# One block of 512 weight columns instead of two of 256 in the first mixer's input projection

## The chip, the cores and the metric

The kernel runs on one core of one Trainium2 chip. Five engines work side by side, each on a queue of its own, in order: PE multiplies matrices (its weight loads are shown apart as PEld), DVE and ACT work element by element, POOL does small odd jobs, SP issues the loads from memory. They wait for one another by semaphores. The metric is the device time of one execution in microseconds; lower is better. Three runs of the kernel before took 1702.97, 1701.64 and 1698.35 us.

## The reference: what is computed

Two layers of a transformer-like trunk over 512 latent and 256 context tokens, width 1024. Each layer is a mixer and a gated feed-forward part, with a normalisation and a shift, scale and gate that come from a conditioning vector ("modulation"). The mixer of layer 0 multiplies the tokens `h` (768 x 1024) by one weight matrix and cuts the result up:

```python
gq, gk, gv, gog, gz, aq, ak, av = _split(h @ w_in, EVEN_SIZES)   # 256 256 512 512 32 512 128 128 columns
# four heads of chunked gated linear attention, in two directions, on gq gk gv gog gz
dirs.append(_directional_scan(q, k, v, g, n_ctx, reverse=(d == 1)))
# and ordinary attention with normalised queries and keys on aq ak av
qa = _rms(aq.reshape(B, N, ATT_KV_HEADS, ATT_GROUP, ATT_HEAD_DIM), att_q_norm)
ka = _rms(ak.reshape(B, N, ATT_KV_HEADS, ATT_HEAD_DIM), att_k_norm)
o_blocks = lax.map(lambda qb: _softmax_attend(qb, k_all, va), q_blocks)
```

The change touches the second half of `aq` (256 columns) and `ak` with `av` (together 256 columns), which lie side by side in the matrix.

## The kernel before, in words

Tokens lie in tiles of 128; tiles 0 to 3 are latent, 4 and 5 context. `even_mixer` is written as a set of generators ("jobs"), each of which does one step when its name comes up in a string of names that `run` walks through (lines 1215 to 1220). The order of PE's instructions in this part is the order of that string: with `self.pinned` set, every matmul is recorded as one that keeps its place (`pin`, line 348). The other engines' queues are put in order by the scheduler, which may move an instruction ahead of others that wait.

The matrix product keeps single precision by splitting both operands in a high and a low part. A block of weights comes in as units of 1024 numbers per partition (`unit`, line 761): a load into a tile `raw` (three buffers), a cast on ACT that makes the high part `wH` (line 769), and a subtraction on DVE that makes the low part `wL` (line 770). There are four buffers of `wH` and four of `wL` for the whole mixer. `nat_units` (line 795) makes the units of a block of columns, `gemm_nat` (line 801) multiplies two token tiles by it: for each of the eight pieces of the inner dimension three matmuls (`h` high by `wH`, `h` high by `wL`, `h` low by `wH`), 48 in all, into a PSUM tile named `nat`. 256 columns need two units of four pieces each.

The job `q` makes the 256 columns of queries that are left, `kv` the keys and values. Each begins with a step that only makes its units, and then has three steps of 48 matmuls, for the tiles 4 and 5, 0 and 1, 2 and 3; after each, ACT copies PSUM to `natq` or `natk` (lines 1138 and 1141). The other names that matter here:

- `v0`, `v1`, `qk0`, `qk1`, `g0`, `g1`: other blocks of the same product. `v0` comes just ahead of `q`; `qk1` (PSUM tile `gqk1`, units of 128 columns) just behind `kv`.
- `m`: the modulation (`mod_vec`, line 515). DVE adds up `macc` from sixteen loaded pieces `mraw`, two instructions each (line 537); then PE sums over partitions (`mod_acc`), DVE copies the sum (`modrows`, line 469), PE turns it (`modT`), DVE adds a bias (`modcol`, line 481). The first of the two rounds goes on: DVE makes `gc` (line 644), PE turns that (`gcT`), DVE copies it (`gt`).
- `c0`: the first job of the gated linear attention, over the context (`gla_job` and `scan`, lines 1256 and 911). It starts with copies and products into `arrg` (lines 1264 to 1267), then goes through levels 1, 2, 4, ... 64: ACT copies a half of `arrg` into `qkg` of that level (line 976), DVE multiplies the half by a decay (line 981), and the next level follows. PE's `pcg` matmuls read the levels 1, 2 and 4 in a first step of `c0`, and 8 and 16 in a second. In names with numbers, `qkg041`, `qkg048` and `qkg0416` are the levels 1, 8 and 16 of this job. `l0` is the same over the latent tokens (`arrg00`).
- `p`: the preparation of queries and keys for attention (`att_prep`), on ACT, DVE and POOL, from `natq` and `natk`.

## Time and profile before

| | us |
|---|---|
| median of three runs | 1701.64 |
| profiled execution | 1703.25 |
| its span in the trace | 1701.1 |
| PE busy | 1650.1 |
| DVE busy | 1309.1 |
| ACT busy | 921.3 |
| mean clock granted to PE | 0.994 |

PE is busy in 97% of the span. Matmuls are pipelined, so a row's duration is longer than the distance to the next matmul: the 128x256 matmuls of `nat` take 0.285 us each and come 0.12 us apart. The chain of waits is read from the end of the program back to its start, at each step to what released it. Stretches where PE has idle time are few; the part of the program that the change touches lies between 95 and 165 us.

### The profile page before, as it was taken

The page shows a single profiled execution, that of the slowest core. Times are in us where ns is not written, and L with a number is a line of the kernel's source. Part 1 is how long each engine was busy: PE and PEld are TensorE (multiplying, and loading weights), DVE is VectorE, ACT ScalarE, POOL GpSimd, SP SyncE. Part 2 cuts the span into 40 slices and gives each one's busy share as a digit, 9 for nine tenths or more (in the row PEclk, how much of TensorE's full clock was granted, in tenths as well). Part 3 has the DMA queues.
Part 4 walks back from the last instruction along what each step waited for, and adds up shares of the span by engine and source line. Part 5 has one row for each costly group of instructions (what it writes and reads, how often), then busy time and mean ns, then how long its engine had stood idle before and what let it go on. Part 6 is the DMA issues. An engine that isn't in the chain of part 4 may idle for free.

```text
span 1701.1 us, 32534 instructions
## 1 busy us (share of the span) xinstructions
PE 1650.1 (97%) x13407; PEld 1484.4 (87%) x13407; DVE 1309.1 (77%) x2102; ACT 921.3 (54%) x1563; POOL 123.2 (7%) x129
## 2 busy tenths in 40 slices
PE   6999998999999999999997999999999999999997
PEld 5899987888999999998886888988888899999875
DVE  5889677976898988777767618788775499987977
ACT  4745567846544444445456326666564565555654
POOL 1004110011000000003101000000000100000221
PEclk9999999999999999999999999999999999999999
DMA  9651012164243454349535612111114334333793
GB/s 327 191 153 40 2 37 90 51 216 158 85 125 111 136 173 142 100 139 197 99 128 194 210 50 63 51 51 51 52 56 156 124 107 118 112 100 100 193 191 136
DMA packets 184736, 204.79 MB, mean 120 GB/s; under 512 B 7142, under 2 KB 141836, under 8 KB 184588
## 3 DMA queue, kind: packets, MB, share of 16 engines
q1 hardware_dynamic: 173632, 181.82, 34.2%
q0 software_dynamic: 9024, 17.30, 5.9%
q10 hardware_dynamic: 1932, 3.59, 0.6%
q8 instruction: 105, 1.72, 0.4%
q14 instruction: 43, 0.35, 0.1%
HBM read 193.23 MB, written 9.46 MB: 119 GB/s over the span
## 4 chain that ended last, share of the span: by engine, by line
PE 81%; DVE 8%; ACT 4%; DMA 3%; issue 2%; POOL 1%; DVEq 0%; SPq 0%; POOLq 0%; ACTq 0%
PE nat L355 12%; PE a L355 11%; PE ff L355 8%; PE E L355 7%; PE x L355 6%; PE oproj L355 6%; PE b L355 4%; PE D L355 4%; PE o L355 4%; PE fq L355 3%; PE gqk L355 2%; PE pearly L355 2%; PE S L355 2%; PE poh L355 1%; PE attO L355 1%
## 5 line engine op out<-in xcount | busy, mean ns | idle before, releaser
L355 PE MATMUL nat<-wH,x 128*128 128x256 f32 (+2 forms) x968 | 224.5, 321 | 3.0 <-ACT x L735 2.6
L355 PEld LDWEIGHTS nat<-wH,x 128*128 128x128 f32 x968 | 162.6, 190 | 19.6 <-ACT x L735 3.7
L824 ACT CAST wH<-raw 128x1024 fp32r<-128x1024 f32 x120 | 125.0, 1051 | 96.5 <-DVE raw L849 33.6
L825 DVE TENSOR_TENSOR wL<-raw,wH 128x1024 fp32r<-128x1024 f32 x120 | 145.6, 1221 | 20.9 <-ACT wH L824 20.3
L355 PE MATMUL nat<-wL,x 128*128 128x256 f32 (+2 forms) x484 | 153.5, 317 | 0.0
L770 DVE TENSOR_TENSOR wL<-raw,wH 128x1024 fp32r<-128x1024 f32 (+1 forms) x83 | 98.7, 1198 | 49.5 <-ACT wH L769 48.5
L355 PE MATMUL ff<-x,wH 128*128 128x512 f32 (+1 forms) x512 | 127.7, 340 | 0.0
L668 POOL TENSOR_TENSOR rs<-ms,neghalf 128x1 f32<-128x1 f32 (+2 forms) x62 | 65.3, 1058 | 785.5 <-DVE ms L666 785.4
L769 ACT CAST wH<-raw 128x1024 fp32r<-128x1024 f32 (+1 forms) x83 | 84.6, 1034 | 67.8 <-PE ff L355 19.8
L355 PE MATMUL oproj<-wH,x 128*128 128x512 f32 x320 | 102.2, 396 | 0.5 <-ACT x L1288 0.4
L355 PEld LDWEIGHTS nat<-wL,x 128*128 128x128 f32 x484 | 92.3, 191 | 5.9 <-DVE wL L770 0.3
L597 DVE SCALAR_TENSOR_TENSOR macc<-mraw,scT,macc 128x1024 f32<-128x1024 f32 x70 | 88.3, 1280 | 11.6 <-DMA mraw<-in_mod_w_dram 11.2
L355 PEld LDWEIGHTS ff<-x,wH 128*128 128x128 f32 x512 | 87.2, 190 | 10.0
L355 PE MATMUL x<-wH,two 128*128 128x512 f32 x280 | 90.5, 392 | 0.9 <-DVE y L1783 0.7
L976 ACT COPY qkh<-arr 128x512 f32<-128x512 f32 x112 | 70.0, 642 | 36.5 <-DVE arr L981 32.1
L1708 POOL DMA_DIRECT2D t<-in_ffn_w_down_dram x36 | 41.8, 1230 | 649.4 <-DVE wL L1742 610.3
L355 PE MATMUL ff<-x,wL 128*128 128x256 f32 (+1 forms) x256 | 86.2, 337 | 0.0
L849 DVE TENSOR_TENSOR raw<-raw 128x512 f32<-128x512 f32 x120 | 82.8, 690 | 2.8
L981 DVE TENSOR_TENSOR arr<-arr,f 128x512 f32<-128x512 f32 x112 | 74.2, 687 | 1.9 <-ACT qkh L976 0.3
L355 PE MATMUL E<-x,wH 128*128 128x384 f32 (+1 forms) x320 | 70.9, 311 | 0.0
L355 PEld LDWEIGHTS oproj<-wH,x 128*128 128x128 f32 x320 | 59.5, 188 | 12.8 <-ACT x L1288 1.0
L355 PE MATMUL b<-x,wH 128*128 128x384 f32 (+1 forms) x320 | 70.5, 309 | 0.0
(422 smaller groups left out, 4548.5 us busy)
## 6 DMA issues: line engine op xcount, KB each, us to landing
mraw<-in_mod_w_dram SPq DMA_DIRECT2D x80, 512.0 KB, 4.5
raw<-in_ffn_w_gate_dram SPq DMA_DIRECT2D x44, 512.0 KB, 4.6
raw<-in_ffn_w_up_dram SPq DMA_DIRECT2D x44, 512.0 KB, 4.1
raw<-in_odd_w_in_dram SPq DMA_DIRECT2D x40, 512.0 KB, 3.8
t<-in_ffn_w_down_dram POOLq DMA_DIRECT2D x30, 512.0 KB, 7.4
raw<-in_ffn_w_down_dram SPq DMA_DIRECT2D x28, 512.0 KB, 7.2
mraw<-in_mod_w_dram SPq DMA_DIRECT2D x32, 256.0 KB, 6.3
raw<-in_even_w_in_dram SPq DMA_DIRECT2D x16, 512.0 KB, 4.0
```

What stands on the lines that cost most here:

```text
L355: return self.pin(self.nc.tensor.matmul(*a, **k))
L597: nc.vector.scalar_tensor_tensor(a, u, w, a, op0=ALU.mult, op1=ALU.add)
L668: nc.gpsimd.tensor_tensor(rs, ms, self.neghalf.to_broadcast([P, w]), op=ALU.pow)
L769: nc.scalar.copy(H[:, :m], raw[:, :m])
L770: nc.vector.tensor_tensor(L[:, :m], raw[:, :m], H[:, :m].bitcast(F32), op=ALU.subtract)
L824: self.nc.scalar.copy(H, f)
L825: self.nc.vector.tensor_tensor(L, f, H.bitcast(F32), op=ALU.subtract)
L849: add = lambda o, x, y: nc.vector.tensor_tensor(o, x, y, op=ALU.add)
L976: nc.scalar.copy(qkv[:, :, :, half, :], dst)
L981: nc.vector.tensor_tensor(dst, dst, tb, op=ALU.mult)
L1708: add = lambda o, src: self.pin(nc.gpsimd.dma_start(out=o, in_=src, accum_op=ALU.add))
```

## The change

The jobs `q` and `kv` become one job `Q` of 512 columns. Its block needs four units of two pieces each instead of two and two of four, and it has three steps of 48 matmuls of 512 columns in place of six steps of 48 matmuls of 256. After each step ACT makes both copies. In the string of names, `Q` stands where `q` stood for the first time (its units) and three more times; `kv` is gone.

```diff
-        def nat(c0, evac):
+        def nat(c0, evac, n=256):
-            us = self.nat_units(w, c0, 256, 0) + self.nat_units(w, c0, 256, 1)
+            us = self.nat_units(w, c0, n, 0) + self.nat_units(w, c0, n, 1)
             yield
             for t0 in tiles:
-                self.gemm_nat(w, c0, 256, h, (t0,), evac, us=us)
+                self.gemm_nat(w, c0, n, h, (t0,), evac, us=us)
                 yield

-        def ev_q(t0, pt):
+        def ev_qkv(t0, pt):
             nc.scalar.copy(q_part(1)[:, t0 : t0 + 2], pt[:, :, :256].rearrange("p t (m e) -> p t m e", m=4))
-
-        def ev_kv(t0, pt):
-            nc.scalar.copy(natk[:, t0 : t0 + 2, :], pt[:, :, :256])
+            nc.scalar.copy(natk[:, t0 : t0 + 2, :], pt[:, :, 256:])

-            "q": lambda: nat(1536 + 288, ev_q), "kv": lambda: nat(1536 + 544, ev_kv), "m": lambda: mods,
+            "Q": lambda: nat(1536 + 288, ev_qkv, 512), "m": lambda: mods,

-        run("qk0 qk0 e m qk0 e e v0 qk0 e e m qk0 e e m v0 e e m m q v0 m m v0 m m kv q m m q m q m m m m m m m m m qk1 kv m")
+        run("qk0 qk0 e m qk0 e e v0 qk0 e e m qk0 e e m v0 e e m m Q v0 m m v0 m m Q m m m m Q m m m m m m m m qk1 m")
         tp.release()
         gp = self.open_pool("gla")
-        run("c0 l0 kv m c0 kv c0 v1 qk1 c0 p p qk1 c0 l0 p qk1 l0 c0 g0 qk1 l0 p c1 p v1 l0 p v1 l0 c1 p v1 l0 c1 l1 g1 g0 c1 g0 r0 c1 l1 r0 g0 l1")
+        run("c0 l0 Q m c0 c0 v1 qk1 c0 p p qk1 c0 l0 p qk1 l0 c0 g0 qk1 l0 p c1 p v1 l0 p v1 l0 c1 p v1 l0 c1 l1 g1 g0 c1 g0 r0 c1 l1 r0 g0 l1")
```

In the built programs the queues differ in a short piece only; from about the place that the kernel before reaches at 165 us, every engine has the same instructions in the same order in both. Three places inside that piece matter below.

On PE, at the first round of the modulation, before (the matmuls of `nat_1168` are the first step of `q`, those of `nat_1234` the second):

```order
L355 MATMUL nat_1168<-wL_1040,x2_356 128x256
L355 MATMUL nat_1168<-wH_1039,x3_357 128x256
L355 MATMUL mod_acc_1218<-macc020_795,one_82 32x512 x2
L355 MATMUL mod_acc_1218<-macc021_796,one_82 32x512 x2
L358 MATMUL modT_1225<-ident_74,modrows_1223 128x128 x4
L355 MATMUL nat_1234<-wH_1033,x0_354 128x256
```

And now (`nat_1168` and `nat_1252` are the first and second step of `Q`):

```order
L355 MATMUL nat_1168<-wL_1052,x2_356 128x512
L355 MATMUL nat_1168<-wH_1051,x3_357 128x512
L355 MATMUL mod_acc_1219<-macc020_795,one_82 32x512 x2
L355 MATMUL mod_acc_1219<-macc021_796,one_82 32x512 x2
L358 MATMUL modT_1226<-ident_74,modrows_1224 128x128 x4
L358 MATMUL gcT02_1235<-ident_74,gc02_1233 16x128
L355 MATMUL nat_1252<-wH_1033,x0_354 128x512
```

The transpose `gcT`, which stood behind the second step of `q`, now stands ahead of the second step of `Q`. In the same way `modT` of the second round, which had the first step of `kv` between itself and its `mod_acc`, now follows it at once, and the third step of `Q` comes behind it.

On DVE at the same place, before:

```order
L537 SCALAR_TENSOR_TENSOR macc031_1292<-mraw034_1355,scT_79,macc031_1292 128x1024
L469 COPY modrows_1223<-mod_acc_1218 128x512
L537 SCALAR_TENSOR_TENSOR macc030_1291<-mraw035_1359,scT_79,macc030_1291 128x1024
L481 TENSOR_TENSOR modcol02_794<-modT_1225,col_84 128x8 x2
L537 SCALAR_TENSOR_TENSOR macc031_1292<-mraw035_1359,scT_79,macc031_1292 128x1024
L644 TENSOR_TENSOR gc02_1232<-modcol02_794,col_84 128x16
```

And now:

```order
L537 SCALAR_TENSOR_TENSOR macc031_1243<-mraw034_1307,scT_79,macc031_1243 128x1024
L537 SCALAR_TENSOR_TENSOR macc030_1242<-mraw035_1311,scT_79,macc030_1242 128x1024
L537 SCALAR_TENSOR_TENSOR macc031_1243<-mraw035_1311,scT_79,macc031_1243 128x1024
L537 SCALAR_TENSOR_TENSOR macc030_1242<-mraw036_1315,scT_79,macc030_1242 128x1024
L537 SCALAR_TENSOR_TENSOR macc031_1243<-mraw036_1315,scT_79,macc031_1243 128x1024
L469 COPY modrows_1224<-mod_acc_1219 128x512
L537 SCALAR_TENSOR_TENSOR macc030_1242<-mraw037_1319,scT_79,macc030_1242 128x1024
L481 TENSOR_TENSOR modcol02_794<-modT_1226,col_84 128x8 x2
L537 SCALAR_TENSOR_TENSOR macc031_1243<-mraw037_1319,scT_79,macc031_1243 128x1024
L644 TENSOR_TENSOR gc02_1233<-modcol02_794,col_84 128x16
```

Four sums of the second round moved ahead of `modrows`; one still stands between `modrows` and `modcol`, and one between `modcol` and `gc`.

On ACT, where the job `c0` has its levels 8 and 16, before (`nat_1501` is the second step of `kv`, `pcg04_1551` and `pcg04_1588` the first step of `c0` on PE):

```order
L1141 COPY natk_648<-nat_1501 128x512
L976 COPY qkg008_2045<-arrg00_1477 128x64x8
L958 ACTIVATE CTg04_1458<-pcg04_1551 128x64
L976 COPY qkg048_1625<-arrg04_1453 128x32x8 x2
L958 ACTIVATE CTg04_1458<-pcg04_1588 128x64
L1320 ACTIVATE rope_1809<-natk_648 128x128
L1320 ACTIVATE rope2_1813<-natq_647 128x512
L976 COPY qkg0416_1631<-arrg04_1453 128x16x16
```

And now (`nat_1403` is the third and last step of `Q`, `wH_1597` a unit of `v1`):

```order
L1138 COPY natq_647<-nat_1403 128x8x64
L1139 COPY natk_648<-nat_1403 128x512
L958 ACTIVATE CTg04_1360<-pcg04_1454 128x64
L1318 ACTIVATE rope2_1666<-natk_648 128x128
L976 COPY qkg008_1898<-arrg00_1379 128x64x8
L976 COPY qkg048_1528<-arrg04_1355 128x32x8
L958 ACTIVATE CTg04_1360<-pcg04_1491 128x64
L976 COPY qkg048_1528<-arrg04_1355 128x32x8
L769 CAST wH_1597<-raw_1596 128x1024
L976 COPY qkg0416_1534<-arrg04_1355 128x16x16 x2
```

The levels 8 and 16, which were made ahead of the last step of `kv`, now stand behind the copies of the last step of `Q`. On PE the four groups of `pcg` stood around the last step of `kv`, two ahead and two behind; now all four follow the last step of `Q`, and `gqk1` follows them.

## The prediction

> **What bounds the kernel now.** I read the page's busy times first, then the chain of waits from 95 to 165 us, where the two orders differ, then the timelines of DVE, ACT and SP there, and last the granted clock around places where PE stood still.

> ```profile
> PE 1650.1 (97%) x13407; PEld 1484.4 (87%) x13407; DVE 1309.1 (77%) x2102; ACT 921.3 (54%) x1563; POOL 123.2 (7%) x129
> ```

> PE is the bound; what counts is its work and each time that it stands still. In the chain (start, duration, what):

> ```profile
> 99.06 3.80 DVE macc L537 x4
> 102.86 0.98 issue
> 103.85 0.69 DVE modrows L469
> 104.54 0.04 issue
> 104.58 0.66 PE modT L358 x4
> 105.24 5.74 PE nat L355 x48
> 110.98 0.11 PE gcT L358
> 111.09 5.74 PE nat L355 x48
> 116.84 0.99 PE mod_acc L355 x8
> 117.83 5.95 PE nat L355 x48
> 123.78 0.44 PE modT L358 x4
> 124.22 5.74 PE nat L355 x48
> 129.96 1.25 PE pcg L355 x83
> 131.21 5.94 PE nat L355 x48
> 137.15 0.69 PE pcg L355 x51
> 137.84 5.66 PE gqk L355 x24
> ```

> From 105.24 on PE runs without a break: five steps of `q` and `kv`, with modulation and `pcg` in between, then `gqk1`. The one stop, before 104.58, is the first modulation: PE had done `mod_acc`, but `modrows` was queued on DVE behind four `macc`. So this stretch is PE's, and every piece of modulation and of `c0` that other engines make is hidden behind a step of `nat`.

> **The change part by part.**

> *PE's own work.* The five rows of 48 above sum to 29.11 us, 5.82 on average; six make 34.9. A 512-wide matmul of the same kind is in the second mixer:

> ```profile
> 952.17 43.56 PE nat L355 x192
> ```

> That is 0.227 us each, 10.9 for 48; with the 0.1 us that a change of tile adds (the difference inside the rows 5.74 and 5.95) 11.0, and 33.0 for three. The gain is 1.9 us, all of it on the path. [...] The rows, 0.227 against twice 0.12, decide.

> *The units.* The third and fourth unit of `Q` are cast where those of `kv` were, after `v0`. Rows of DVE (second number: duration):

> ```profile
> 96.79 2.35 DVE L770 TENSOR_TENSOR wL<-raw,wH 128x1024 fp32r<-128x1024 f32 x2
> 99.06 4.87 DVE L537 SCALAR_TENSOR_TENSOR macc<-mraw,scT,macc 128x1024 f32<-128x1024 f32 x4
> 105.64 0.23 DVE L481 TENSOR_TENSOR modcol<-modT,col 128x8 f32<-128x8 f32 x2
> 106.98 0.17 DVE L644 TENSOR_TENSOR gc<-modcol,col 128x16 f32<-128x16 f32 x1
> 117.90 0.69 DVE L469 COPY modrows<-mod_acc 128x512 f32<-128x512 f32 x1 [0.16 <-PE mod_acc L355]
> 119.64 0.42 DVE L1266 TENSOR_TENSOR arrg<-gqk,glaf 128x256 f32<-128x256 f32 x1
> ```

> The low parts are ready at 98.0 and 99.1. `Q` starts at 95.8 and wants them after 12 and 18 matmuls, at 98.7 and 100.1: no wait. SP issues the same loads in the same order up to here.

> *First modulation.* `mod_acc` now comes when the first step of `Q` ends:

> ```profile
> 101.69 1.06 PE L355 MATMUL mod_acc<-macc,one 128*32 128x512 f32 x8
> ```

> so at 101.6 + 11.0 - 5.8 = 106.8, and ends at 107.85. DVE has four more `macc` ahead of `modrows` and is done with them at 103.85 + 4 x 1.2 = 108.65; `modT` follows 0.73 later (103.85 to 104.58), at 109.4. DVE meanwhile begins the next `macc` at 109.25, so `modcol` waits until 110.45, `gc` for one more `macc`, until 111.8. `gcT` has lost its cover: it was behind a step of `q`, now the second step of `Q` is behind it and starts at 112.15. From 106.8 that is 5.35 us; before, 101.6 to 105.0 and 0.1 for `gcT`, 3.5. Cost 1.85.

> *Second modulation.* `mod_acc` ends at 112.15 + 11.0 + 1.0 = 124.15; `modT` now follows at once and waits 0.75 for `modrows` (DVE is idle). The third step of `Q` starts at 125.35 and ends at 136.35. Cost 0.7.

> *`c0`.* Before, DVE and ACT began it at 118.3 to 119.6. Now it stands behind `modrows` and behind the copies of the second step of `Q`, so it begins at 124.1 to 124.8, 5.5 us later. The casts of `qk1` and `v1` stand in the middle of it on ACT, each waiting until PE has read the buffer for the last time in the third step (at 132.0, 133.4 and 134.8). Levels 1, 2 and 4 come by 130, before they are wanted at 136.4; that part of `pcg` ends at 137.7. Levels 8 and 16 stand behind the copies of the third step, which can start at 136.45. The durations, from ACT before:

> ```profile
> 130.33 0.58 ACT L1141 COPY natk<-nat 128x512 f32<-128x512 f32 x1
> 130.81 0.62 ACT L976 COPY qkg<-arrg 128x512 f32<-128x512 f32 x1
> 131.33 0.23 ACT L958 ACTIVATE CTg<-pcg 128x64 f32<-128x64 f32 x1
> 131.45 0.71 ACT L976 COPY qkg<-arrg 128x256 f32<-128x256 f32 x2
> 132.05 0.23 ACT L958 ACTIVATE CTg<-pcg 128x64 f32<-128x64 f32 x1
> 132.17 0.31 ACT L1320 ACTIVATE rope<-natk 128x128 f32<-128x128 f32 x1
> 137.67 1.05 ACT L769 CAST wH<-raw 128x1024 fp32r<-128x1024 f32 x1
> 138.62 0.71 ACT L976 COPY qkg<-arrg 128x256 f32<-128x256 f32 x2
> ```

> By the distance to the next start: two copies 0.48 each, `CTg` 0.12, a square 0.2, level 8 of `l0` 0.52, level 8 of `c0` 0.3, `CTg` 0.12, 0.3, the cast of `wH_1597` 0.95, level 16 0.7: 4.2 us, to 140.65. PE still has three quarters of 0.69 to do, so `gqk1` starts at 141.3 in place of 137.8: 3.5 us late. Of that 2.9 are a wait that was not there, since the sum of the other terms (-1.9 + 1.85 + 0.7) is 0.65.

> *What comes after.* Levels 32 and 64 need two copies and two products each, of about 0.35 us, in turn: some 3 us more, to 143.7; `gqk1` covers them, since it runs 5.66 us from 141.3. DVE also has rope work and the states of `c0` late, by the 5.5 us that `c0` began later, which is 2 us more than PE is late; `gqk1` and the matmuls behind it cover that, so it costs nothing. If this cover failed, PE would wait for the difference, up to 2 us. From about 165 us the orders are equal, so what PE has lost by then goes through to the end.

> *The clock.* Windows (span, length, PE busy, granted clock, DMA):

> ```profile
> 102.80:104.50 1.70, 0.00 (x0) 1.00 1.05 337
> 104.60:108.00 3.40, 3.40 (x29) 1.00 0.63 235
> 259.20:261.20 2.00, 0.01 (x1) 1.00 0.68 197
> 261.60:264.90 3.30, 3.30 (x21) 0.50 0.90 293
> 265.10:268.00 2.90, 1.46 (x12) 1.00 0.93 367
> ```

> A stop of 1.7 us changed nothing; one of 2.0 us was followed by 3.3 us at half clock, which costs up to 1.7. The new stops are longer: idle 1.55 and 2.2 us around `modT`, and 2.9 us ahead of `gqk1`. How much of the slow 3.4 us falls on matmuls depends on where it begins; between 0 and 1.7 I take 1.4 for the first, where some 0.6 us falls on the stop itself, and 1.2 for the second, where the stop may also be split between two periods. [...]

> Sum: -1.9 + 1.85 + 0.7 + 2.9 + 1.4 + 1.2 = +6.1 us. The profiled execution took 1703.25 us and would take 1709.4; the median of the three runs stands 1.6 lower, so I forecast 1701.64 + 6.1 = 1707.7.

> **Rivals.**

> *Clock slowed once:* the second stop is split by the periods, as that at 103 us may have been. +4.9: 1706.5. *Never:* +3.5: 1705.1. For these speaks that 0.50 followed only stops of 2 us or more with little work around; against, that the first modulation's stops stand only 0.4 us apart.

> *Not slower:* `c0` isn't late. The scheduler's place for the copies of level 16 matters only if ACT really reaches them after PE; should they be ready by 137.7, 2.95 us ahead of my sum, there is no stop before `gqk1`, and with no half clock +0.6 is left: 1702.3. Against it, PE has to deliver the third step before ACT can pass its copies, and behind these stand 3.2 us of rows. If the first modulation were hidden too, -1.2.

> *The transfer decides:* `raw_1596` for the cast ahead of level 16 needs the buffer that DVE's `wL_1334` frees, at about 134.85, and then lands 4.0 us later:

> ```profile
> 117.77 25.41 SPq L768 DMA_DIRECT2D raw<-in_even_w_in_dram  x4
> DMA to landing us min/median/max: 4.0/4.0/4.0
> ```

> That is 138.95, just when ACT comes to the cast (139.0): no slack. DVE late by 2 us adds 2, for 1709.7; every further us one more. For it speaks that DVE has no gap from 126 on in the new order.

> **How the numbers follow.** Three runs spread by 4.6 us, so 0.3% (5.1 us) is about what a measurement can tell from no change. Forecast 0.42 (1706.2 to 1709.2 by itself, each slow period between 0.8 and 1.7); clock slowed once 0.23; never 0.12; late transfer 0.14; not slower 0.09. Over +5.1 lie most of the forecast (0.36), 0.06 of the second and 0.13 of the transfer: slower 0.55. Beyond -5.1 lies none of these cases, since the whole gain is 1.9; 0.03 for what I have not seen. Within 0.3%: 0.42. The range reaches down to the case without half clock with a spread of the runs below it, and up to the late transfer with its 2 us: 1703 to 1712.

> **What would show it.** In the new chain: three rows of 48 `nat` of about 10.9 us; a gap of 5.3 us between the first two with `gcT` at its end, waiting on DVE `gc`; 0.75 us on `modrows` ahead of the third; a wait of PE `pcg` on ACT `qkg` of about 2.9 us; `gqk1` at 141 to 144; and windows at 0.50 behind the stops. I am wrong if `pcg` does not wait, if the queues catch up so that the attention after 220 us begins less than 3 us late, or if a unit of `Q` is late and the first row of `nat` is longer than 11.2.

## The result, and the profile after

The changed kernel takes 1712.2 us (median of six runs, 1711.62 to 1713.06), the kernel before 1701.27 (six runs beside it, 1698.35 to 1702.97): the ratio is 1.0063, 95% interval 1.0052 to 1.0074. The change costs 10.9 us, against 6.1 forecast. The profiled execution after took 1711.62 us with a span of 1709.7; that of before had 1701.1. So the pair of traces shows 8.6 of the 10.9 us; more on the rest below.

The page's busy times after:

```profile
PE 1653.3 (97%) x13263; PEld 1480.6 (87%) x13263; DVE 1309.1 (77%) x2102; ACT 921.1 (54%) x1563; POOL 121.7 (7%) x129
```

PE has 144 matmuls fewer and yet is busy 3.2 us longer: at half clock (below) a 512-column matmul of `nat` is busy for 0.63 us (113.82), at full clock for 0.39 (118.44). DVE and ACT do what they did. The chain of waits of the changed kernel where the orders differ (start, duration, what):

```profile
102.06 5.22 DMA mraw<-in_mod_w_dram
...
107.37 1.96 DVE macc L537 x2
...
109.77 0.68 DVE modrows L469
...
112.99 0.10 DVE gc L644
...
113.59 12.97 PE nat L355 x48
126.56 1.04 PE mod_acc L355 x8
...
127.62 0.70 DVE modrows L469
...
128.37 0.66 PE modT L358 x4
129.03 10.93 PE nat L355 x48
...
142.61 0.94 ACT wH L769
143.55 0.62 ACT qkg L976 x2
...
144.21 0.63 PE pcg L355 x45
144.84 7.28 PE gqk L355 x24
```

Before, this stretch was handed over once, at the first modulation, and was PE's from 105.24 us on. Now it is handed over three times: to DVE before the second step of `Q`, to DVE again before the third, to ACT between the third step and `gqk1`. PE's own timeline shows the waits, and who ended them:

```profile
107.52 1.06 PE L355 MATMUL mod_acc<-macc,one 128*32 128x512 f32 x8
110.51 0.67 PE L358 MATMUL modT<-ident,modrows 128*128 128x128 f32 x4 [1.93 <-DVE modrows L469]
113.22 0.37 PE L358 MATMUL gcT<-ident,gc 128*16 128x128 f32 x1 [2.04 <-DVE gc L644]
...
143.23 0.33 PE L355 MATMUL pcg<-qkg 64*32 64x32 f32 x16 [2.04 <-DVE CTg L961]
144.21 0.63 PE L355 MATMUL pcg<-qkg 64*32 64x32 f32 x48 [0.65 <-ACT qkg L976]
```

And windows laid on the stops and what follows (span, length, PE busy, PEld, DVE, ACT, POOL, granted clock, DMA):

```profile
107.50:111.00 3.50, 1.57 (x13) 0.58 (x12) 3.50 (x4) 1.07 (x2) 0.00 (x0) 1.00 0.13 52
111.10:117.80 6.70, 4.66 (x13) 3.63 (x13) 2.25 (x6) 0.00 (x0) 0.00 (x0) 0.50 0.01 1
141.30:145.10 3.80, 1.22 (x65) 1.06 (x66) 3.70 (x14) 3.80 (x11) 1.97 (x1) 1.00 0.82 237
145.20:148.50 3.30, 3.30 (x10) 2.53 (x9) 3.30 (x15) 1.54 (x6) 0.00 (x0) 0.50 0.74 206
```

Behind the first stop the clock is at a half for 6.8 us (the window leaves out the edges), twice the stretch that the prediction read from the trace of before; behind the third for 3.4 us. The second step of `Q` takes 12.97 us where the third takes 10.93, and `gqk1` 7.28 where it took 5.66.

### The profile page after: what moved, and what is told of

It reads as the page before. It is cut to its first block, busy times and chain, and to the rows that moved or that the text cites. A ratio compares the mean times of both kernels' runs of the same rounds, so it can differ in the third digit from the quotient of the medians.

```text
span 1709.7 us, 32248 instructions
## 1 busy us (share of the span) xinstructions
PE 1653.3 (97%) x13263; PEld 1480.6 (87%) x13263; DVE 1309.1 (77%) x2102; ACT 921.1 (54%) x1563; POOL 121.7 (7%) x129
## 4 chain that ended last, share of the span: by engine, by line
PE 83%; DVE 7%; ACT 4%; DMA 3%; issue 2%; POOL 1%; DVEq 0%; SPq 0%; POOLq 0%; ACTq 0%
PE a L355 12%; PE nat L355 11%; PE ff L355 8%; PE E L355 8%; PE x L355 7%; PE oproj L355 6%; PE o L355 4%; PE D L355 4%; PE b L355 4%; PE fq L355 3%; PE gqk L355 2%; PE pearly L355 2%; PE S L355 2%; PE attO L355 1%; PE poh L355 1%
## 5 line engine op out<-in xcount | busy, mean ns | idle before, releaser
L355 PE MATMUL nat<-wH,x 128*128 128x256 f32 (+2 forms) x872 | 221.0, 339 | 3.2 <-ACT x L735 2.6
L355 PEld LDWEIGHTS nat<-wH,x 128*128 128x128 f32 x872 | 151.7, 191 | 23.2 <-ACT x L735 3.7
L355 PE MATMUL nat<-wL,x 128*128 128x256 f32 (+2 forms) x436 | 146.2, 335 | 0.0
L770 DVE TENSOR_TENSOR wL<-raw,wH 128x1024 fp32r<-128x1024 f32 (+1 forms) x83 | 98.6, 1198 | 47.0 <-ACT wH L769 46.1
L355 PE MATMUL ff<-x,wH 128*128 128x512 f32 (+1 forms) x512 | 127.6, 340 | 0.0
L769 ACT CAST wH<-raw 128x1024 fp32r<-128x1024 f32 (+1 forms) x83 | 84.7, 1035 | 66.8 <-PE ff L355 20.1
L355 PE MATMUL oproj<-wH,x 128*128 128x512 f32 x320 | 102.3, 396 | 0.5 <-ACT x L1286 0.4
L355 PEld LDWEIGHTS ff<-x,wH 128*128 128x128 f32 x512 | 87.3, 190 | 10.0
L355 PE MATMUL x<-wH,two 128*128 128x512 f32 x280 | 90.5, 392 | 0.9 <-DVE y L1781 0.7
L355 PEld LDWEIGHTS nat<-wL,x 128*128 128x128 f32 x436 | 83.5, 192 | 7.8 <-DVE wL L770 0.3
L976 ACT COPY qkh<-arr 128x512 f32<-128x512 f32 x112 | 70.1, 642 | 36.3 <-DVE arr L981 32.2
L355 PE MATMUL ff<-x,wL 128*128 128x256 f32 (+1 forms) x256 | 86.2, 337 | 0.0
L355 PE MATMUL E<-x,wH 128*128 128x384 f32 (+1 forms) x320 | 70.9, 311 | 0.0
L355 PE MATMUL a<-T,wH 128*128 128x384 f32 (+1 forms) x320 | 70.4, 309 | 0.3 <-ACT qb L887 0.3
L355 PE MATMUL b<-x,wH 128*128 128x384 f32 (+1 forms) x320 | 70.6, 309 | 0.0
```

The source lines that it names most:

```text
L355: return self.pin(self.nc.tensor.matmul(*a, **k))
L769: nc.scalar.copy(H[:, :m], raw[:, :m])
L770: nc.vector.tensor_tensor(L[:, :m], raw[:, :m], H[:, :m].bitcast(F32), op=ALU.subtract)
L976: nc.scalar.copy(qkv[:, :, :, half, :], dst)
```

## The experiments

**The places of before, with 512 columns.** Is the wide block itself worth what the sum says, if modulation and `c0` keep their places? Each step of `Q` is cut in two half steps of 24 matmuls, one token tile each, and these stand where the six steps of before stood.

```diff
+                for a in range(2):
+                    tok = slice((t0 + a) * P, (t0 + a + 1) * P)
+                    for k in range(KD):
+                        W = us[k // 2]
+                        self.mm3(pt[:, a, :], h.hl(k, tok), (W[0][:, k % 2, :], W[1][:, k % 2, :]), k == 0, k == KD - 1)
+                    if a:
+                        ev_qkv(t0, pt)
+                    yield
-        run("... Q v0 m m v0 m m Q m m m m Q m m m m m m m m qk1 m")
+        run("... Q v0 m m v0 m m Q m m Q m Q m m m m m m m m m qk1 Q m")
-        run("c0 l0 Q m c0 c0 v1 qk1 c0 p p ...
+        run("c0 l0 Q m c0 Q c0 v1 qk1 c0 p p ...
```

> The block of 512 columns in six half steps, one token tile each (24 matmuls of 512 columns, copies after the second half), at the six places where the kernel before has the steps of q and kv. Theory (the stops came only from the three long steps): no new stop, what is left is the gain of the wide matmuls, 1.9 us: 1701.3 - 1.9 = 1699.4 us, ratio 0.999, at most one new wait of under 1 us on a cast of qk1, since its buffers come free only in the last half step. Rival (the four units held until the end cost by themselves): 1705 us or more, with PE waiting for wH or wL ahead of gqk1.

Measured: 1699.88 us, ratio 0.9992 (0.9983 to 1.0001); run once more, 1700.28 us, ratio 0.9991 (0.9983 to 1.0000).

> The kernel of half steps again, on the same chip at the same time as the filled one: 1699.9 with its ratio to the kernel before within 0.9983 to 1.0001 as in its first run; the slow stretches at other places of the 3.41 us grid.

From 104.36 us on its chain of waits has PE rows without a break, with half steps where the steps of 256 columns stood:

```profile
104.36 5.47 PE nat L355 x24
...
109.94 5.48 PE nat L355 x24
115.42 0.99 PE mod_acc L355 x8
...
134.93 0.69 PE pcg L355 x51
135.61 5.68 PE gqk L355 x24
```

The five half steps from 104.36 on, of 5.47 to 5.67 us, sum to 27.8 us where those of before sum to 29.1: 1.3 us, or 1.6 over six, against 1.9 worked out. The medians are 1.3 and 0.8 us under those of before, with intervals that just reach no change. So the wide block's own gain is small: the rows show it, and both runs point the same way without settling it. What the change loses doesn't come from the wide block; that leaves the order.

**The order alone, with 256 columns.** The counterpart: every step of `Q` is made as one step of `q` and one of `kv`, both 256 wide, with the order of the changed kernel.

```diff
+        def nat2(cq, ck):
+            uq = self.nat_units(w, cq, 256, 0) + self.nat_units(w, cq, 256, 1)
+            uk = self.nat_units(w, ck, 256, 0) + self.nat_units(w, ck, 256, 1)
+            yield
+            for t0 in tiles:
+                self.gemm_nat(w, cq, 256, h, (t0,), ev_q, us=uq)
+                self.gemm_nat(w, ck, 256, h, (t0,), ev_kv, us=uk)
+                yield
...
-            "Q": lambda: nat(1536 + 288, ev_qkv, 512), "m": lambda: mods,
+            "Q": lambda: nat2(1536 + 288, 1536 + 544), "m": lambda: mods,
```

> The order of the changed kernel with matmuls of 256 columns: each step of Q is made as 48 matmuls for the queries and then 48 for keys and values, in the units of the kernel before; the order of the names is that of the changed kernel. Theory (the order makes the stops, the wide matmuls by themselves gain): the stops stay, the gain of 1.9 us is lost, so 1712.2 + 1.9 = 1714 us, ratio to before about 1.0075, with gcT and pcg waiting as in the changed kernel. Rival (the block of 512 columns costs by itself, through its four units held at once or the wide matmuls): near the kernel before, 1701 to 1704 us. A second rival, half of each: 1707.

Measured: 1710.55 us, ratio 1.0053 (1.0040 to 1.0066). The order by itself costs 9.4 us, most of what the change costs. It took 3.4 us less than expected, and isn't slower than the changed kernel, though its third step takes 0.6 us more (11.52 against 10.93). Its second step, 12.98, had a shorter slow stretch, 3.4 us for 6.8:

```profile
113.87 12.98 PE nat L355 x96
...
129.31 11.52 PE nat L355 x96
```

From the first `logit` to the first `oproj` matmul its trace is 0.4 us longer than the changed kernel's (287.5 for 287.1). The rest of the miss lies later, where the kernels are equal.

**One stop at a time.** From the kernel of half steps, only the first modulation is put where the change puts it (behind a whole step); or only the second modulation and `c0`.

```diff
-        run("... m m Q m m Q m Q m m m m m m m m m qk1 Q m")
+        run("... m m Q Q m m m Q m m m m m m m m m qk1 Q m")
```

```diff
-        run("... m m Q m m Q m Q m m m m m m m m m qk1 Q m")
+        run("... m m Q m m Q m Q Q m m m m m m m m m qk1 m")
-        run("c0 l0 Q m c0 Q c0 v1 ...
+        run("c0 l0 Q Q m c0 c0 v1 ...
```

> Only the first modulation stands as in the changed kernel (behind a whole step of 512, gcT ahead of the second step); the second modulation and c0 stand between half steps as before. Theory (each place costs by itself): 1699.9 + 2.6 of longer stop + 2.1 of half clock in the steps behind it = 1704.6, no gap ahead of gqk1. Rival (the first stop makes c0 late as well): a gap ahead of gqk1 and 1708 or more.

> Only the second modulation and the first levels of c0 stand as in the changed kernel (whole 512-wide step between them); the first modulation stands at the places of before, between half steps. Theory (each place costs by itself): against the kernel of half steps (1699.9) it loses the second modulation's stop (about 1.0), the stop ahead of gqk1 (2.9), the half clock behind it (1.6) and 0.7 of small waits, so 1706.1; against the changed kernel (1712.2) it gains 2.6 of the first stop and 2.1 of half clock, so 1707.5; I expect 1706.8 and a row of gqk1 of about 7.3 us behind a gap of 4 to 5 us. Rival (c0 is late only because the first modulation held DVE and PE up): no gap ahead of gqk1, 1701 to 1702.

Measured: the first alone 1704.83 us (ratio 1.0020, 1.0011 to 1.0029), the second alone 1706.32 (1.0025, 1.0014 to 1.0036). Against 1699.88 that is +4.9 and +6.4, together 11.3; the changed kernel is 12.3 above it. The two runs came within 0.5 us of what was expected (1704.6 and 1706.8). The two places cost by themselves, and the rival, that one lateness makes the other, is out. The chain of the first alone shows the half clock in its first half step (7.06 for 5.5) and no wait ahead of `gqk1`:

```profile
112.70 7.06 PE nat L355 x24
119.76 0.99 PE mod_acc L355 x8
120.76 5.67 PE nat L355 x24
...
139.27 0.69 PE pcg L355 x51
139.95 5.68 PE gqk L355 x24
```

That of the second alone shows the wait, from the end of the last step at 134.13 to `gqk1` at 139.01, and the half clock behind it:

```profile
123.21 10.92 PE nat L355 x48
...
138.38 0.63 PE pcg L355 x45
139.01 7.27 PE gqk L355 x24
```

**The stops without half clock.** In the three stops of the changed kernel PE is given 6, 7 and 9 further matmuls of 512 columns.

```diff
-... m m Q m m m m Q m m ...            c0 l0 Q m c0 c0 v1 ...
+... m m Q m w m w m m Q m m ...        c0 l0 Q m c0 w c0 v1 ...
+        def warm():
+            H = h.hl(0, slice(0, 512))[0]
+            for n in (6, 7, 9):
+                pt = self.mm_tile("warm")
+                for i in range(n):
+                    self.mm(pt[:, :512], H[:, :P], H, start=True, stop=True)
+                yield
...
+            "w": warm,
```

> The changed kernel with 22 matmuls of 512 columns whose results nobody reads, put in PE's order into the three stops (6 behind the first mod_acc, 7 behind its modT, 9 between the two parts of pcg), as much as fits into the idle time. Theory (the half clock after the stops costs 2.0 us in the second step of Q, 12.97 in place of 10.9, and 1.6 in the first part of gqk1, 7.28 in place of 5.66): the clock stays at 1.00 there, both rows go back to 10.9 and 5.7, and the time falls by 3.6 us to 1708.6, the stops being as long as they were. Rival (the longer rows come from something else, such as the copies or the loads at the same time): no fall, 1712 or a little more.

Measured: 1705.34 us, ratio 1.0023 (1.0015 to 1.0032), 6.9 us under the changed kernel. The stops are still there (the second step of `Q` starts at 113.25 for 113.59), but the same windows of the trace stand at full clock, and the step behind the first stop has its normal length (windows, then chain):

```profile
111.10:117.80 6.70, 6.27 (x29) 4.89 (x28) 2.01 (x6) 0.00 (x0) 0.00 (x0) 1.00 0.01 1
145.20:148.50 3.30, 3.30 (x32) 2.52 (x34) 3.30 (x9) 0.83 (x2) 2.30 (x3) 1.00 0.14 47
```

```profile
113.25 10.89 PE nat L355 x48
```

**`c0` one step later.** If the wait ahead of `gqk1` is only a matter of `pcg` standing too early in PE's queue, moving that step behind the first part of `gqk1` removes it.

```diff
-        run("c0 l0 Q m c0 c0 v1 qk1 c0 p p ...
+        run("c0 l0 Q m c0 v1 qk1 c0 c0 p p ...
```

> The changed kernel with the second pcg step of c0 (levels 8 and 16) moved behind the first part of gqk1 in the order of names, so that gqk1 covers the wait. Theory: the third stop (2.7 us idle ahead of gqk1) and the half clock after it (1.6) go: 1712.2 - 4.3 = 1707.9 us. Rival (ACT and DVE are behind as a whole, and the stop only moves on to pbg or to the next pcg): 1711 to 1712.5 us, with a new wait of PE of 2 to 3 us between 145 and 170 us.

Measured: 1712.54 us, ratio 1.0066 (1.0053 to 1.0080), no gain, as the rival has it. PE's timeline shows the stop one job further, ahead of `pbg`, and a half clock behind it again (151.7 to 155.0 us):

```profile
150.30 0.68 PE L355 MATMUL pbg<-qkg 64*64 64x64 f32 x16 [2.80 <-ACT qkg L976]
151.42 0.85 PE L355 MATMUL pbg<-qkg 64*64 64x64 f32 x14 [0.44 <-DVE CTg L961]
```

`c0` as a whole comes late, since its first copies stand behind the second modulation; the place of one reader doesn't change that. An earlier start of `c0` would, which this order doesn't allow; with the half steps, where `c0` starts earlier, the wait is gone.

**The changed kernel once more.** Does the half clock fall the same way in every execution?

> The changed kernel once more, one look. Theory (slow periods lie on a grid of 3.41 us whose place differs from execution to execution): the first mixer's rows are as in the first look within 0.5 us (second step of Q 12.5 to 13.5, gqk1 7.0 to 7.6), but the slow stretches begin at other places, and the time from the first oproj to the end differs from the first look's 1358.3 us by up to 3 us. Rival (the later clock is fixed by the kernel): it differs by less than 0.5 us.

Measured: span 1710.8 us. The third stop's row is alike (7.16), but the step behind the first stop takes 12.53 in place of 12.97, with one slow stretch in place of two:

```profile
112.60 12.53 PE nat L355 x48
...
143.46 7.16 PE gqk L355 x24
```

From the first `oproj` (350.2) to the end it takes 1360.6 us, 2.3 more than in the first execution. That is within the 3 us expected, but not for the reason given, the clock: at the long stop of the second layer the second execution had one slow period less and gained 0.4 us there. Compared matmul by matmul, it lost 2.7 us near 700, near 1370 to 1400 and near 1630 us.

**Filling another stop.** There is a stop of about 7 us at the start of the second layer's values, with half clock around it (0.85 on average from 915 to 950 us in the second run of the half steps); that run, in the chain:

```profile
928.91 3.78 PE hT L355 x16
932.69 11.98 PE nat L355 x48
```

Undisturbed these rows would be about 1.95 and 10.9, as the sixteen `hT` at 921.41 and the 48 `nat` at 932.98 in the last run below. Into that stop (in `pair_turn`, ahead of the third quarter) go 26 further 512-column matmuls, on top of the half steps.

```diff
+                if q == 2 and self.fill:
+                    pf, self.fill = (self.sc_tile("fill", 0), self.fill), None
+                    for i in range(26):
+                        self.mm(pf[0], *pf[1], start=True, stop=True)
...
                         if c == 0 and x in (0, 2):
+                            if x == 0:
+                                self.fill = h1.hl(0, slice(order[0] * P, order[0] * P + P))[0], value(0, 0)[0][:, 0, :]
                             self.turn_next()
```

> The kernel of half steps (1699.9) with 26 more 512-column matmuls in the 7 us stop at the start of the second layer's values (between the second and third quarter of a turn, about 925 us); their result is read by nobody. Theory (the stop, not the work, brings half clock, and the half clock costs 1.4 to 2.9 us there by where the periods fall): 1697.9, hT behind the stop at 1.95 us in place of 3.4, no granted clock under 1 between 915 and 950. Rival (the added matmuls only delay hT or the slow periods come at the next stop instead): 1699.9 or more.

Measured: 1700.53 us, ratio 0.9993 (0.9984 to 1.0001), no gain. The clock stayed full (1.00 from 910 to 960 us), but the timeline of PE shows two waits in `nat` that weren't there:

```profile
956.93 0.73 PE L355 MATMUL nat<-wH,x 128*128 128x512 f32 x2 [2.94 <-DVE x L740]
959.58 0.74 PE L355 MATMUL nat<-wH,x 128*128 128x512 f32 x2 [1.00 <-DVE x L740]
```

and DVE's timeline why: the scheduler had put three more `macc` ahead of the low part `x` of the third pair, and these waited for their transfers:

```profile
952.51 3.76 DVE L597 SCALAR_TENSOR_TENSOR macc<-mraw,scT,macc 128x1024 f32<-128x1024 f32 x3 [2.35 <-DMA mraw<-in_mod_w_dram]
956.19 0.68 DVE L740 TENSOR_TENSOR x<-hf,x 128x512 fp32r<-128x512 f32 x1
```

So the late modulation is held back until the last `x` is made, but for its first two steps:

```diff
-        self.nc.vector.tensor_tensor(L, f, H.bitcast(F32), op=ALU.subtract)
+        self.low = self.nc.vector.tensor_tensor(L, f, H.bitcast(F32), op=ALU.subtract)
...
+                early = [True] * 2
...
-                    with self.tc.issue_after(self.mark.ins):
-                        for _ in range(n):
+                    for _ in range(n):
+                        with self.tc.issue_after((self.mark if early else self.low).ins):
                             next(mods, None)
+                        if early:
+                            early.pop()
```

> The kernel of half steps with the 26 filling matmuls once more (their result is read by nobody); new is that all but the first two steps of the late modulation are issued behind the last low part of h1, so that no macc waiting for its transfer stands ahead of x on DVE. Theory (the filling did save the half clock, 1.4 us, and the two waits of nat on DVE x, 2.9 and 1.0 us, took it back): no such waits between 943 and 960, no granted clock under 1 between 915 and 950, 1697.5 to 1698.5, 1.4 to 2.4 under the half-step kernel run beside it. Rival (something else holds the second layer, such as mod_acc and gcT ahead of ff at 1000 us): 1699.5 to 1700.5, as the half-step kernel.

Measured: 1696.6 us, ratio 0.9973 (0.9961 to 0.9985), against 1700.28 for the half steps beside it. It is the fastest of all, 4.5 us under the kernel before. Its window over the whole place, and its chain:

```profile
915.00:950.00 35.00, 33.12 (x175) 27.63 (x174) 15.40 (x25) 21.29 (x40) 2.68 (x5) 1.00 0.40 136
```

```profile
931.82 1.16 PE hT L355 x8
932.98 10.93 PE nat L355 x48
...
948.49 43.55 PE nat L355 x192
```

No wait of `nat` is left. Of the 3.7 us gained, the stop gives 2.2 in this pair of traces: from the first `hT` of the turn to the end of the step of 48 it took 24.7 us with half clock and takes 22.5 now. Against the first trace of the half steps, where that stop had two slow periods for three, it would be 0.8. The rest falls near 1354 and near 1622 us, where executions of one kernel differ too. Holding the modulation back was not run without the filling; from 948 to 1300 us this trace and that of the half steps keep their distance, so nothing there speaks for a gain of its own.

## Why the prediction was right in its sign and short in its size

Slower was the likeliest of the three outcomes and came; the 10.9 us are 4.8 above the forecast, and 1712.2 lies just over the range's upper end of 1712. Of the 4.8, 1.8 are terms of the sum, 0.7 what comes after, and 2.3 stay open. Each term, from the traces (before against after):

| term | forecast | measured |
|---|---|---|
| PE's own work | -1.9 | -2.1 (three steps of 10.93 for 34.9) |
| first modulation's stop | +1.85 | +2.4 (107.52 to 113.59, less 101.69 to 105.24 and 0.11 for `gcT`) |
| half clock behind it | +1.4 | +2.04 (12.97 - 10.93) |
| second modulation | +0.7 | +1.04 (126.56 to 129.03, less 0.99 + 0.44) |
| wait ahead of `gqk1` | +2.9 | +2.94 (139.96 to 144.84, less 1.25 + 0.69) |
| half clock behind it | +1.2 | +1.62 (7.28 - 5.66) |
| sum | +6.1 | +7.9 |

The sum can be taken from the trace as well: `gqk1` ends at 152.12 for 143.50, 8.6 us later, of which 0.7 was there before the orders part (the first `logit` starts at 64.3 for 63.6; over all traces between 63.6 and 64.7, so this is the execution, not the change).

- *The steps of `Q`, their units, the gain of 512 columns.* Right: 10.93 forecast as 10.9, no unit late; the half steps at the old places give the gain by itself. Over six half steps 1.6 us were measured, over three whole ones 2.1, for the 1.9 worked out from the rows.
- *First modulation.* The mechanism was right, with `gcT` at its end; the term was mis-sized by 0.55. DVE was to run through its four `macc` without a break, but the next piece `mraw` landed 5.22 us after its issue and DVE stood for 0.55. (The gap of before, 3.5 in the prediction, is 3.66 by its rows; the new one is 6.07 for 5.35.) In the second execution the piece landed after 4.82 us, and the term is 2.0.
- *Second modulation.* The wait for `modrows` was right (0.77 for 0.75). Missed by 0.3: `modT`, with nothing beside it, takes 0.66 us of the path in place of 0.44.
- *`c0`.* Right to 0.1 us, and by the chain that was worked out: copies of the third step, levels 8, the cast of `wH`, level 16, `pcg`. The rival that the transfer decides didn't come about; `wH` was cast at 142.6 without a wait for it.
- *The clock.* Both stops did slow it, so the rivals with one or no slow period are out. The term was mis-sized by 0.6 and 0.4: it took the first stop to be followed by one period of 3.4 us, some of which falls on the stop. In this execution there were two, 6.8 us, the first of which lies mostly over the stop (it begins at 111.0, and the step at 113.59). The second execution had one, and 0.44 us less in that row. The prediction also took no account of how much PE worked within a slow period (last section): the first of the two had PE busy for 40% (1.37 of 3.41 us), and a second followed; the one of the second execution lay on the step, PE busy throughout (3.41 of 3.41), and none followed. That the 2.0 us stop read from the trace of before was followed by half clock was luck: the same stop, 2.1 us by PE's timeline, was followed by full clock in four of the twelve traces.
- *What comes after.* "It costs nothing" was wrong by 0.7: `oproj` begins at 351.4 for 342.1, which is 8.6 later without the 0.7 that was there at the start. PE loses the difference in two places, 0.3 us near 172 and 0.4 near 216 us; the trace names nothing that PE waited for there, so the cause stays open.
- *The rest.* Of the 10.9 us in the medians, the stretch up to `oproj` accounts for 8.6. The remaining 2.3 stay open. From `oproj` on the kernels are equal, yet this stretch took between 1355.8 and 1360.6 us in the traces of the kernels that don't differ in it. Before and after happened to be alike there in the profiled pair (1359.0 and 1358.3), where the one execution was 2.0 us above its median and the other 0.6 below. One trace of each can't say how much of that is the change's.

## What to carry to other kernels

The wider matmuls saved 1.6 to 2.1 us here, but a wider step is also a longer one, and every short job that was hidden behind a short step may lose its cover: look at what stands between the steps before merging them, and if need be cut the wide step along the tokens so that the old places stay. Count with the clock behind a stop of PE, and not only with the stop: here half clock followed one and the same stop of 2.1 us in eight of twelve traces, for 3.41 us in that of the kernel before. Other matmuls in the stop took the half clock away in the three runs that had them (1.00 for 0.50), not the stop itself. When PE gets faster or its order changes, look again at the in-order queues that feed it: an instruction that waits for a transfer, put ahead of one that PE wants, can give the gain back, as two waits of 2.94 and 1.00 us did here (1700.53 us for 1696.6).

## What the runs showed of the hardware

From 60 to 1690 us the stretches at half clock were 3.4, 6.8 or 10.2 us long in these traces: in that of the kernel before 3.41 us at 261.56 and 10.24 at 927.16, in that of the changed kernel 6.83 at 111.02, 3.41 at 145.15, 3.41 at 271.44 and 10.24 at 937.04. Within the one execution their starts are multiples of 3.413 us apart: 10, 37 and 195 times from one to the next in the changed kernel's (826.02 us, 242 times, from the first to the last), 195 times in that of before. The second execution of the changed kernel has its first one at 112.50.

Cut into steps of 3.413 us from these starts, the traces show how busy PE was ahead of each change of the clock:

| trace | step from | clock | PE busy | clock in the next step |
|---|---|---|---|---|
| before | 101.13 | 1.00 | 48% | 1.00 |
| before | 258.15 | 1.00 | 38% | 0.50 |
| before | 923.75 | 1.00 | 39% | 0.50 |
| before | 930.57 | 0.50 | 55% | 0.50 |
| before | 933.99 | 0.50 | 100% | 1.00 |
| changed | 107.61 | 1.00 | 43% | 0.50 |
| changed | 111.02 | 0.50 | 40% | 0.50 |
| changed | 114.43 | 0.50 | 100% | 1.00 |
| changed | 141.74 | 1.00 | 37% | 0.50 |
| changed | 940.46 | 0.50 | 75% | 0.50 |
| `c0` one step later | 933.31 | 1.00 | 45% | 1.00 |
| half steps, first run | 929.53 | 0.50 | 83% | 1.00 |

In the traces of before and after, between 60 and 1690 us, none of the steps at full clock that half clock followed had PE busy for more than the 43% at 107.61, and none of the others for less than the 48% at 101.13. And the same stop was followed by half clock in one execution and not in another: that of 2.1 us in the attention, in the kernel before (half clock followed) and in the run with the first modulation alone (none followed; windows of one step: span, length, PE busy, granted clock, DMA):

```profile
258.15:261.56 3.41, 1.31 (x12) 1.00 0.72 237
```

```profile
260.38:263.79 3.41, 1.68 (x12) 1.00 0.63 201
```

And the slow period at the first modulation in the two executions of the changed kernel, the first with little of the step in it (a second slow period followed), the other full (none did):

```profile
111.02:114.43 3.41, 1.37 (x6) 0.50 0.00 0
```

```profile
112.50:115.91 3.41, 3.41 (x10) 0.50 0.01 2
```

These shares are read from the traces named; no run moved a stop along the steps by itself.

The long stop of the second layer differed too: it had three slow periods in the changed kernel (10.24 us) and two in the run with filled stops (6.83 us), 1.4 us less. But the number of periods there doesn't order the times of the stretch behind `oproj`: with three it took 1356.9 to 1359.4 us, with two 1355.8 to 1360.6. So it is one source among others of the differences between executions.

In the first mixer of the changed kernel half clock began behind a stop of PE of 1.93 us (at 111.02, within `modT`; the 2.04 us behind `modT` lie in it), and behind stops of 2.04 and 0.65 us ahead of `gqk1` (at 145.15).
